# A hybrid decoder block in float32: the first block's first input tile is loaded ahead of the weights, and one retention head moves within block 3

## The chip, the cores and the metric

The kernel runs on one core of a Trainium2 chip. TensorE (PE, with its weight loads PEld), VectorE (DVE), ScalarE (ACT) and GpSimd (POOL) compute, each an instruction stream that is executed in order; SyncE (SP) issues most of the transfers, ScalarE a few, and both streams of transfers are also issued in order. The metric is the device time of one execution in microseconds, as the median of several runs.

## The reference

```python
n = rms_norm(h, attn_norm_w)
proj = einsum('bsd,dc->bsc', n, w_in)
(gq, gk, gv, gg, ga, gb, rq, rk, rv, rg) = split(proj)
o_gdn = gated_deltanet(gq, gk, gv, gg, ga, gb, ...)   # 4 heads, chunked recurrence over the sequence
o_ret = retention(rq, rk, rv, rg)                      # 4 heads, fixed decay per head
h = h + einsum('bsm,md->bsd', concat([o_gdn, o_ret]), w_out)
n2 = rms_norm(h, mlp_norm_w)
h = h + einsum('bsf,fd->bsd', silu(conv(n2 @ w_up)_g) * conv(n2 @ w_up)_u, w_down)
return rms_norm(h, final_norm_w)
```

The sequence has 2048 rows of 1024 columns, heads have 128 columns, the MLP has 2816 hidden columns. Everything is float32.

## The kernel before

**Products.** Each float32 operand is split into a rounded high part (ACT copies it to float32r) and the rest (DVE subtracts), and each product is three TensorE matmuls: high by high, high by low, low by high. `mm3` (lines 113 to 118) records them, as do lines 399 to 401. The output projection and the MLP are done as seven products of half-size blocks (a Winograd form): `product(i)` (line 907) is one of the seven of the output projection, in the order 1, 2, 6, 7, 5, 3, 4.

**Stages.** The sequence is cut into four blocks of 512 rows. For each block the mixers run (projections, gated DeltaNet, retention), then the output projection with its residual and the second norm. After the four blocks follow the MLP's up products and the MLP's down products.

**The order.** The string `ORDER` (lines 41 to 51) lists the items of the four blocks as they are recorded: a digit for the block, then a name. `pro` loads the block's rows and splits them (`pro2` loads the transposed rows `xT` in four tiles `xk` of two k-slices each, line 382, and makes the scaled split tiles `n1`; `pro1` loads the plain rows and takes their squares). `k0`, `v0`, `q0`, `kq` are retention projections, `a`, `f` DeltaNet projections. `r10` to `r13` are four steps of the DeltaNet recurrence of heads 2 and 3 (`gdn_rec`), each a chain that goes TensorE (`ks`), VectorE (line 717), TensorE (`wps`), VectorE (line 727), TensorE (`sps`), VectorE (line 734). `h3` is `ret_head(3)` (transposes `rtr`, products `rkk` and `rr`), `y3` is `ret_out(3)` (the products `ro`, their copy on ACT and the squares). `g0`, `g1` and `G0`, `G1` are `gated(g, hf)` for the first and second half of a block: VectorE multiplies the gate (line 435), TensorE transposes (`mxt`, line 437), ACT copies the result into `co` or `og` (line 440), and for the second half VectorE makes the sums `co[5]`, `co[6]`, `co[7]`, `co[3]` (lines 442 to 445). `W1` is `product(1)`; it reads the first half of the DeltaNet heads, `W2` the first half of the retention heads, `W6` and later ones the sums. A product loads four weight tiles `wv` (five buffers), splits its operand `wu` for two halves m, and records 24 matmuls `wo`.

**What is done with that order.** The items are recorded in this order, each weight load one item ahead (`load_chunk`, called in `hybrid_block`, lines 140 to 150), and a scheduler in the framework then reorders instructions on every engine by its own estimates, within the dependences. So a change of the recorded order can move instructions that it does not name. In the stage between block 3 and the MLP the scheduler lays the MLP's first input splits (`x_...<-xr`, lines 973 and 974, whose loads `xr` SP issues), the remaining output projection and the MLP's first matmuls (`p`) over each other. `unit` (line 72) hands out fixed-size buffers of a pool.

**Weights at the start.** The first item with weights is `0k0`: 264 columns, four loads `wraw` of two k-slices each (line 293), three buffers, split into eight tiles `wc` (lines 295 and 296).

Of the kernel before, what the change touches and what calls it, by code (L numbers as in the profile page):

```python
# [51 lines left out]
P = 128  # L52
S = 2048
D = 1024
# [1 line left out]
TB = 512  # L56
# [15 lines left out]
def unit(pool, tag, shape, dt=F32, **kw):  # L72

    n = int(np.prod(shape[1:]))
    t = pool.tile([P, U1], dt, tag=tag, name=tag, **kw)[:, :n]
    if len(shape) == 3:
        t = t.rearrange("p (a b) -> p a b", a=shape[1])
    elif len(shape) == 4:
        t = t.rearrange("p (a b c) -> p a b c", a=shape[1], b=shape[2])
    return t  # L80


@with_exitstack
def hybrid_block(ctx, tc, x, xT, w_kq, w_v, w_g, w_rk, w_r0, w_r, w_o, w_u, w_d, cols, rows, fnr, masks, rot, out):
    nc = tc.nc
    PE, ACT, DVE, POOL = nc.tensor, nc.scalar, nc.vector, nc.gpsimd

    cp = ctx.enter_context(tc.tile_pool(name="cp", bufs=1))
    drp = ctx.enter_context(tc.tile_pool(name="drp", bufs=2, space=DRAM))


    NCOL = cols.shape[1]
    base = cp.tile([P, U1], F32, name="base")
    colt = base[:, :NCOL]
    nc.scalar.dma_start(colt, cols)
    n1w = colt[:, 0:8]
    n2w = colt[:, 8:16]
    gcw = colt[:, 16:64].rearrange("p (f t) -> p f t", t=4)
    mcw = colt[:, 64:64 + 132].rearrange("p (f t) -> p f t", t=3)
    gv127 = colt[:, 196:200]  # L100
    epsr = colt[:, 200:204]
    gnw = colt[:, 204:205]
    mhalf = base[:, NCOL:NCOL + 16]
    POOL.memset(mhalf, -0.5)
    o = NCOL + 16
    mhalo = base[:, o:o + 4 * NF].rearrange("p (f t) -> p f t", t=2)
    o += 4 * NF
    sfa = base[:, o:o + 2 * (S // P)].rearrange("p (a b) -> p a b", b=2)
    o += 2 * (S // P)

    gamma = [1.0 - 2.0 ** (-5 - h) for h in range(NH)]

    def mm3(ps, pairs, first=True, chk=False):
        n = len(pairs)
        for i, (ah, al, bh, bl) in enumerate(pairs):
            PE.matmul(ps, ah, bh, start=(first and i == 0), stop=False, skip_group_check=chk)  # L116
            PE.matmul(ps, ah, bl, start=False, stop=False, skip_group_check=chk)  # L117
            PE.matmul(ps, al, bh, start=False, stop=(i == n - 1), skip_group_check=chk)  # L118


    n2d = {(b, kk): drp.tile([2, P, TB], F32, name=f"n2d{b}_{kk}", tag=f"n2d{b}_{kk}", bufs=1)
           for b in range(NB) for kk in range(4)}
    hd = [drp.tile([TB, D], F32, name=f"hd{b}", tag=f"hd{b}", bufs=1) for b in range(NB)]
    wud = {}
    marks = {}
    aud = {(q, i): drp.tile([NP, P, TB], F32, name=f"au{q}_{i}", tag=f"au{q}_{i}", bufs=1)
           for q in range(2) for i in range(1, 8)}

    items = mixers(ctx, tc, base, o, marks, drp, mm3, gamma, mhalf, n1w, n2w, gcw, gv127, epsr, gnw, n2d, hd,
                   x, xT, w_kq, w_v, w_g, w_rk, w_r0, w_r, w_o, rows, masks, rot)  # L130
    ups = mlp_up(ctx, tc, marks, drp, mm3, mcw, mhalo, n2d, wud, aud, w_u)
    seq = []
    for name in ORDER.split():
        seq += [(None, None, None)] if name == "U" else items[int(name[0])][name[1:]]
    load_chunk = items["load"]
    order = [i for i, it in enumerate(seq) if it[0] is not None]
    loaded = {}
    nxt = 0
    done = 0
    for i, it in enumerate(seq):  # L140
        while nxt < len(order) and nxt <= done + LA:
            loaded[order[nxt]] = load_chunk(*seq[order[nxt]][:2])
            nxt += 1
        if it[0] is not None:
            it[2](loaded.pop(i))
            done += 1
        elif it[2] is None:
            next(ups)
        else:
            it[2](None)  # L150
    for _ in ups:
        pass
    mlp_down(tc, marks, drp, mm3, sfa, mhalf, hd, aud, w_d, fnr, out)
# [65 lines left out]
def mixers(ctx, tc, base, base_used, marks, drp, mm3, gamma, mhalf, n1w, n2w, gcw, gv127, epsr, gnw, n2d, hd,  # L219
           x, xT, w_kq, w_v, w_g, w_rk, w_r0, w_r, w_o, rows, masks, rot):  # L220
    nc = tc.nc
# [3 lines left out]
    ap_ = ctx.enter_context(tc.tile_pool(name="ap"))  # L225
# [89 lines left out]
    def al(tag, shape, dt=F32):  # L315
        return unit(ap_, tag, shape, dt, **({"bufs": BUFS[tag]} if tag in BUFS else {}))
# [38 lines left out]
    def A_items(b, st):  # L355
# [22 lines left out]
        def pro2(_):  # L378
            st["n1"] = []
            for kk in range(4):  # L380
                xk = unit(ap_, "xk0", [P, 2, TB], bufs=4) if b == 0 else al("xk", [P, 2, TB])
                nc.sync.dma_start(xk.rearrange("p a t -> p (a t)"), xT[b, kk])
                for i in range(2):
                    k = 2 * kk + i
                    n1 = al("n1", [P, 2, TB], F32R)
                    st["n1"].append(n1)
                    ACT.activation(n1[:, 0], xk[:, i], AF.Copy, scale=n1w[:, k:k + 1])  # L387
                    DVE.scalar_tensor_tensor(n1[:, 1], xk[:, i], n1w[:, k:k + 1], n1[:, 0].bitcast(F32),
                                             op0=ALU.mult, op1=ALU.subtract)
# [481 lines left out]
        def gt(g):  # L871
            return [(("g", g), w_g[g], gates(g))]

        items = {"pro": [(None, None, pro2), (None, None, pro1)], "dec": [(None, None, decays)]}
        for h in range(NH):
            items.update({f"d{h}": [(None, None, dmat(h))], f"a{h}": [(("kq", h), w_kq[h], proj_kq(h))],
# [6 lines left out]
        return items  # L883

    wvc = {}

    def W_items(b):
        C = {}
# [68 lines left out]
    sts = [dict() for _ in range(NB)]  # L957
    items = {b: A_items(b, sts[b]) | W_items(b) for b in range(NB)}
    items["load"] = load_chunk
    return items  # L960


# [372 lines left out]
```

## Time and profile before

| what | value |
|---|---|
| median of 3 runs | 2459.84 us (2457.41 to 2461.82) |
| the profiled execution, whole | 2460.31 us |
| its span, first to last instruction | 2458.5 us |
| TensorE's mean granted clock in it | 0.996 |
| VectorE, ScalarE, GpSimd busy | 65%, 41%, 22% |

The profile is of one execution. In its rows "idle before" is the time that an engine stood still ahead of an instruction, with the instruction that released it; PEclk is the share of TensorE's full clock that was granted. Matmuls overlap, so the duration printed for one is longer than the distance between the starts of two.

### The profile page before, as it was taken

The page shows a single profiled execution, that of the slowest core. Times are in us where ns is not written, and L with a number is a line of the kernel's source. Part 1 is how long each engine was busy: PE and PEld are TensorE (multiplying, and loading weights), DVE is VectorE, ACT ScalarE, POOL GpSimd, SP SyncE. Part 2 cuts the span into 40 slices and gives each one's busy share as a digit, 9 for nine tenths or more (in the row PEclk, how much of TensorE's full clock was granted, in tenths as well). Part 3 has the DMA queues.
Part 4 walks back from the last instruction along what each step waited for, and adds up shares of the span by engine and source line. Part 5 has one row for each costly group of instructions (what it writes and reads, how often), then busy time and mean ns, then how long its engine had stood idle before and what let it go on. Part 6 is the DMA issues. An engine that isn't in the chain of part 4 may idle for free.

```text
span 2458.5 us, 35801 instructions
## 1 busy us (share of the span) xinstructions
PE 2397.2 (98%) x12476; PEld 2016.0 (82%) x12476; DVE 1596.7 (65%) x3157; ACT 998.8 (41%) x2152; POOL 532.7 (22%) x877
## 2 busy tenths in 40 slices
PE   8998899999999999998999999999999999999998
PEld 7887788788888878887888888888888888888887
DVE  5855777444754563447888988896556577454674
ACT  6644535344442552336454344442122234332341
POOL 1354245621047105240000000000000002421030
PEclk9999999999999999999999999999999999999999
DMA  8856589674765656654998878877667778775773
GB/s 327 277 187 218 214 310 343 223 247 175 268 228 180 211 186 222 224 184 181 349 365 313 303 290 300 290 280 250 233 239 258 270 259 281 243 224 156 220 242 112
DMA packets 287477, 607.29 MB, mean 247 GB/s; under 512 B 41088, under 2 KB 121152, under 8 KB 287296
## 3 DMA queue, kind: packets, MB, share of 16 engines
q1 hardware_dynamic: 270720, 590.70, 68.7%
q10 hardware_dynamic: 16576, 14.30, 1.9%
q8 instruction: 98, 1.61, 0.3%
q14 instruction: 83, 0.68, 0.1%
HBM read 405.32 MB, written 199.59 MB: 246 GB/s over the span
## 4 chain that ended last, share of the span: by engine, by line
PE 84%; POOL 5%; DMA 4%; DVE 3%; issue 2%; ACT 2%; SPq 0%; ACTq 0%; POOLq 0%; DVEq 0%
PE p L116 11%; PE p L118 11%; PE p L117 11%; PE d L118 6%; PE d L116 6%; PE d L117 6%; PE tok L399 4%; PE tok L401 4%; PE tok L400 4%; PE chm L116 3%; PE chm L117 3%; PE chm L118 3%; POOL pers L639 2%; POOL pers L637 2%; PE wo L116 2%; PE wo L117 2%
## 5 line engine op out<-in xcount | busy, mean ns | idle before, releaser
L117 PE MATMUL p<-x,wu 128*128 128x512 f32 x1176 | 457.7, 389 | 0.0
L116 PE MATMUL p<-x,wu 128*128 128x512 f32 x1176 | 452.7, 389 | 0.0
L118 PE MATMUL p<-x,wu 128*128 128x512 f32 x1176 | 450.0, 389 | 0.0
L399 PE MATMUL tok<-wc,n 128*128 128x512 f32 (+2 forms) x768 | 276.5, 365 | 19.5 <-ACT n L387 9.6
L400 PE MATMUL tok<-wc,n 128*128 128x512 f32 (+2 forms) x768 | 276.6, 361 | 1.1 <-DVE wc L296 1.1
L401 PE MATMUL tok<-wc,n 128*128 128x512 f32 (+2 forms) x768 | 275.1, 361 | 0.0
L116 PEld LDWEIGHTS p<-x,wu 128*128 128x128 f32 x1176 | 220.8, 188 | 46.4 <-DVE uc L1053 0.4
L118 PEld LDWEIGHTS p<-x,wu 128*128 128x128 f32 x1176 | 220.8, 188 | 45.8
L117 PEld LDWEIGHTS p<-x,wu 128*128 128x128 f32 x1176 | 220.8, 188 | 45.8
L1095 DVE SCALAR_TENSOR_TENSOR acc<-uc,base,acc 128x1023 f32<-128x1023 f32 (+1 forms) x176 | 221.0, 1280 | 39.2 <-ACT acc L1092 38.9
L1053 DVE TENSOR_TENSOR uc<-p,uc 128x512 f32<-128x512 f32 x224 | 153.6, 689 | 134.8 <-PE p L118 131.6
L186 POOL TENSOR_TENSOR vt<-vr 128x512 f32<-128x512 f32 x44 | 66.0, 1504 | 633.0 <-DMA vr<-in_w_d 465.8
L399 PEld LDWEIGHTS tok<-wc,n 128*128 128x128 f32 x768 | 146.1, 191 | 41.0 <-ACT n L387 9.6
L117 PE MATMUL d<-v,uu 128*128 128x512 f32 x448 | 174.3, 389 | 0.0
L118 PE MATMUL d<-v,uu 128*128 128x512 f32 x448 | 174.3, 389 | 0.0
L116 PE MATMUL d<-v,uu 128*128 128x512 f32 x448 | 174.3, 389 | 0.0
L400 PEld LDWEIGHTS tok<-wc,n 128*128 128x128 f32 x768 | 146.5, 191 | 20.8 <-DVE wc L296 1.5
L401 PEld LDWEIGHTS tok<-wc,n 128*128 128x128 f32 x768 | 145.3, 191 | 19.8
L116 PE MATMUL chm<-n,wc 128*128 128x512 f32 x384 | 151.7, 395 | 0.0
L118 PE MATMUL chm<-n,wc 128*128 128x512 f32 x384 | 151.2, 394 | 0.0
L117 PE MATMUL chm<-n,wc 128*128 128x512 f32 x384 | 150.8, 393 | 0.0
L1092 ACT ACTIVATE acc<-uc,base 128x1024 f32<-128x1024 f32 x88 | 97.2, 1144 | 86.2 <-DVE uc L1053 45.1
(250 smaller groups left out, 4723.3 us busy)
## 6 DMA issues: line engine op xcount, KB each, us to landing
wu<-wu SPq DMA_DIRECT2D x308, 512.0 KB, 5.9
wc<-wd SPq DMA_DIRECT2D x168, 512.0 KB, 5.2
wv<-wo SPq DMA_DIRECT2D x84, 512.0 KB, 5.2
wd<-wc SPq DMA_DIRECT2D x60, 512.0 KB, 4.8
ur<-au SPq DMA_DIRECT2D x56, 512.0 KB, 5.5
wur<-in_w_u SPq DMA_DIRECT2D x44, 512.0 KB, 6.5
au<-st SPq DMA_DIRECT2D x88, 256.0 KB, 4.7
vr<-in_w_d SPq DMA_DIRECT2D x77, 256.0 KB, 5.0
```

The costliest lines, as they stand in the source:

```text
L116: PE.matmul(ps, ah, bh, start=(first and i == 0), stop=False, skip_group_check=chk)
L117: PE.matmul(ps, ah, bl, start=False, stop=False, skip_group_check=chk)
L118: PE.matmul(ps, al, bh, start=False, stop=(i == n - 1), skip_group_check=chk)
L186: POOL.tensor_tensor(tt[:, j], a, b_, op=ALU.subtract)
L399: PE.matmul(ps, ah, wh, start=(k == 0), stop=False)
L400: PE.matmul(ps, ah, wl, start=False, stop=False)
L401: PE.matmul(ps, al_, wh, start=False, stop=(k == KT - 1))
L637: POOL.tensor_tensor(tm[:, :, :n], Nb[:, j:j + 1, j + 1:].to_broadcast([P, 8, n]), X[:, :, j:j + 1].to_broadcast([P, 8, n]), op=ALU.mult)
L639: POOL.tensor_tensor(X[:, :, j + 1:], X[:, :, j + 1:], tm[:, :, :n], op=ALU.add)
L1053: add = lambda o, ps, a: DVE.tensor_tensor(o, ps, a, op=ALU.add)
L1092: ACT.activation(acc, u, AF.Copy, scale=mcw[:, ci, 2:3])
L1095: DVE.scalar_tensor_tensor(acc[:, t:], u[:, :T2 - t], w, acc[:, t:], op0=ALU.mult, op1=ALU.add)
```

## The change

Two things are changed. A function `load_first` allocates the first of block 0's four `xk` buffers and issues its load; `hybrid_block` calls it ahead of the loop that records the items and loads the weights, and `pro2` takes that tile in place of loading its own. In `ORDER` the items `3h3 3y3` stand between `3r11` and `3r12`, where they stood behind `2N`.

```diff
-         "2W3 3a3 3c3 3kq 3y1 3f3 3e3 3p0 3l0 3r00 3r01 3r02 3r03 3h2 3y2 3b1 3l1 3r10 3r11 3r12 3r13 "
-         "3g0 2W4 3p1 3G0 2N 3h3 3y3 3g1 3G1 3W1 3W2 3W6 3W7 3W5 3W3 3W4 3N")
+         "2W3 3a3 3c3 3kq 3y1 3f3 3e3 3p0 3l0 3r00 3r01 3r02 3r03 3h2 3y2 3b1 3l1 3r10 3r11 3h3 3y3 3r12 "
+         "3r13 3g0 2W4 3p1 3G0 2N 3g1 3G1 3W1 3W2 3W6 3W7 3W5 3W3 3W4 3N")
...
     ups = mlp_up(ctx, tc, marks, drp, mm3, mcw, mhalo, n2d, wud, aud, w_u)
+    items["first"]()
     seq = []
...
             for kk in range(4):
-                xk = unit(ap_, "xk0", [P, 2, TB], bufs=4) if b == 0 else al("xk", [P, 2, TB])
-                nc.sync.dma_start(xk.rearrange("p a t -> p (a t)"), xT[b, kk])
+                if b == 0 and kk == 0:
+                    xk = first[0]
+                else:
+                    xk = unit(ap_, "xk0", [P, 2, TB], bufs=4) if b == 0 else al("xk", [P, 2, TB])
+                    nc.sync.dma_start(xk.rearrange("p a t -> p (a t)"), xT[b, kk])
...
+    first = []
+
+    def load_first():
+        xk = unit(ap_, "xk0", [P, 2, TB], bufs=4)
+        first.append(xk)
+        nc.sync.dma_start(xk.rearrange("p a t -> p (a t)"), xT[0, 0])
...
+    items["first"] = load_first
```

No instruction is added or removed on TensorE, VectorE, GpSimd or SP; ACT gets two more loads of its function table. What the scheduler makes of it differs in two stretches, the first 90 us and the stretch from 1104 us on, and is the same between.

**SP, the first transfers of the program.** `wraw` are the weight loads of `0k0` (`in_w_rk`) and of `0v0` (`in_w_r`), `xk<-in_xT` the four transposed input tiles, `xk<-in_x` the plain rows, `wvr` and `wx` loads for the output projection. Before:

```order
L293 DMA wraw<-in_w_rk 128x528 x2
L382 DMA xk_198<-in_xT 128x1024
L293 DMA wraw<-in_w_rk 128x528
L382 DMA xk_206<-in_xT 128x1024
L382 DMA xk_214<-in_xT 128x1024
L382 DMA xk_222<-in_xT 128x1024
L293 DMA wraw<-in_w_rk 128x528
L360 DMA xk<-in_x 128x1024
L293 DMA wraw<-in_w_r 128x1024
```

Now:

```order
L896 DMA xk_134<-in_xT 128x1024
L294 DMA wraw<-in_w_rk 128x528 x2
L386 DMA xk_206<-in_xT 128x1024
L294 DMA wraw<-in_w_rk 128x528
L386 DMA xk_214<-in_xT 128x1024
L386 DMA xk_222<-in_xT 128x1024
L361 DMA xk<-in_x 128x1024 x2
L179 DMA wvr<-in_w_o 128x512
L294 DMA wraw<-in_w_rk 128x528
L179 DMA wvr<-in_w_o 128x512
L294 DMA wraw<-in_w_r 128x1024
```

The first input tile stands ahead of the first two weight loads, and the fourth weight load of `0k0` stands behind two loads of plain rows and one `wvr`.

**TensorE, the end of block 3's mixers.** `ro` is the last part of `3y3`, `sps` and `ks` are parts of a recurrence step, `nps` is `2N`; `wo` on `wu_11715` and `wu_11737` is `3W1`, on `wu_11765` and `wu_11782` `3W2`, on `wu_11807` and `wu_11824` `3W6`. Before, behind the whole of `3W1` and the last recurrence step:

```order
L846 MATMUL ro<-rv,Ar 128x128
L847 MATMUL ro<-pers_662,ykq 128x128
L437 MATMUL mxt<-base,mix 128x128 x10
L116 MATMUL wo<-wv,wu_11765 128x512
L117 MATMUL wo<-wv,wu_11765 128x512
L116 MATMUL wo<-wv,wu_11782 128x512
```

Now the products of head 3 stand a step earlier, ahead of the last one and of `3W1`:

```order
L963 MATMUL nps<-base,Cw 128x128 x4
L728 MATMUL wps<-kv,AT 128x128 x2
L736 MATMUL sps<-pers_1350,kv 128x128 x2
L736 MATMUL sps<-pers_1350,AT 128x128 x2
L822 MATMUL rr<-rv,rk 128x128 x4
L850 MATMUL ro<-rv,Ar 128x128
L851 MATMUL ro<-pers_125,ykq 128x128
```

and the last eight transposes of the mixers stand between the end of `3W2` and the start of `3W6`:

```order
L118 MATMUL wo<-wv,wu_11765 128x512
L116 MATMUL wo<-wv,wu_11782 128x512
L117 MATMUL wo<-wv,wu_11782 128x512
L118 MATMUL wo<-wv,wu_11782 128x512
L441 MATMUL mxt<-base,mix 128x128 x8
L116 MATMUL wo<-wv,wu_11807 128x512
L117 MATMUL wo<-wv,wu_11807 128x512
L116 MATMUL wo<-wv,wu_11824 128x512
```

So `3W2`, 24 matmuls, was behind the last transposes and is now ahead of them.

**ACT, the copies of those last transposes.** `co` and `og` are the copies of the transposes, `x_2` and `x_3` splits of the MLP's input, `wu_...<-co` the operands of the products. Before:

```order
L440 ACTIVATE og<-mxt,base 128x256
L440 ACTIVATE co<-mxt 128x256
L973 ACTIVATE x_3_12274<-xr 128x512
L440 ACTIVATE co<-mxt 128x256 x2
L917 ACTIVATE wu_11765<-co 128x512
L917 ACTIVATE wu_11782<-co 128x512
L440 ACTIVATE og<-mxt,base 128x256
```

Now:

```order
L444 ACTIVATE co<-mxt 128x256
L444 ACTIVATE og<-mxt,base 128x256
L444 ACTIVATE co<-mxt 128x256
L985 ACTIVATE x_2_12259<-xr 128x512
L985 ACTIVATE x_3_12274<-xr 128x512
L444 ACTIVATE og<-mxt,base 128x256
L928 ACTIVATE wu_11807<-co 128x512
```

The operand splits of `3W2` (`wu_11765`, `wu_11782`) no longer stand among these copies but ahead of them, and the operand of `3W6` follows the last copy directly.

## Prediction

> **What bounds the kernel now.** I read the page first, then TensorE's waits, then the stretches of time in which they lie. The page:
>
> ```profile
> PE 2397.2 (98%) x12476; PEld 2016.0 (82%) x12476; DVE 1596.7 (65%) x3157; ACT 998.8 (41%) x2152; POOL 532.7 (22%) x877
> ```
>
> TensorE is busy for 98%, so only its 61 us of idle time (2458.5 less 2397.2), and time at a reduced clock, can be won by a change that removes no matmul. The waits of TensorE over the whole span (engine and line, what it waited for, us in total, times, longest), its five largest:
>
> ```profile
> PE tok L399 <- ACT n L387: 9.6, 1, 9.6
> PE sps L732 <- DVE pers L727: 6.4, 11, 0.9
> PE mxt L437 <- DVE mix L435: 5.8, 2, 5.0
> PE tok L399 <- ACT mix L412: 5.4, 1, 5.4
> PE wps L724 <- DVE kv L717: 4.8, 8, 1.4
> ```
>
> The first is the start of the program, the third is mostly one wait at the end of block 3, the second and the last are the DeltaNet recurrence. The change reorders just the start and the end of block 3. The stretch at the end of block 3, cut into the recurrence up to its last `ks`, the part up to the last `ro`, and the part up to the first matmul of `3W6` (length, then busy time of PE, PEld, DVE, ACT, POOL, then PEclk, DMA share, GB/s):
>
> ```profile
> 1104.73:1133.74 29.01, 25.20 (x212) 23.26 (x211) 20.07 (x67) 17.01 (x58) 4.04 (x4) 1.00 0.20 73
> 1133.74:1145.14 11.40, 10.95 (x70) 9.59 (x68) 5.75 (x16) 5.12 (x17) 0.50 (x1) 1.00 0.46 147
> 1145.14:1162.92 17.78, 11.64 (x42) 9.44 (x43) 15.61 (x36) 12.90 (x31) 1.51 (x2) 0.71 0.83 313
> ```
>
> Idle there: 3.8, 0.45 and 6.1 us, together 10.4 us. The third part also ran at a mean clock of 0.71. TensorE's rows in it, and two other gaps with the clock around them:
>
> ```profile
> 1150.18 2.37 PE L437 MATMUL mxt<-base,mix 128*128 128x128 f32 x10 [5.05 <-DVE mix L435]
> 1153.64 0.79 PE L116 MATMUL wo<-wv,wu 128*128 128x512 f32 x1 [1.09 <-ACT wu L917]
> 1158.08 0.43 PE L118 MATMUL wo<-wv,wu 128*128 128x512 f32 x1
> 1158.35 0.40 PE L116 MATMUL wo<-wv,wu 128*128 128x512 f32 x1
> 1158.58 0.40 PE L117 MATMUL wo<-wv,wu 128*128 128x512 f32 x1
> ...
> 151.98 1.13 PE L585 MATMUL kk<-ykq 128*128 128x256 f32 x4 [2.35 <-DVE pers L810]
> 218.32 0.80 PE L399 MATMUL tok<-wc,n 128*128 128x512 f32 x1 [5.43 <-ACT mix L412]
> ```
>
> ```profile
> 150.00:155.00 5.00, 3.02 (x13) 2.56 (x14) 4.53 (x9) 4.87 (x17) 2.30 (x3) 1.00 0.82 321
> 215.00:220.00 5.00, 1.68 (x4) 1.39 (x5) 0.00 (x0) 1.57 (x4) 2.46 (x10) 0.61 0.08 26
> 1150.00:1155.00 5.00, 3.72 (x13) 3.16 (x14) 5.00 (x13) 4.90 (x12) 0.00 (x0) 0.50 0.85 329
> ```
>
> A gap of 2.35 us left the clock at 1.00; gaps of 5.43 and 5.05 us halved it. From 1153.64 to 1158.08 ten `wo` took 4.44 us, where the distance at full clock is 0.23 us (1158.35 to 1158.58): 2.1 us lost. The ten transposes before took 2.37 us, about 1.3 us more than at full clock. So the stretch loses 10.4 + 2.1 + 1.3 = 13.8 us in all.
>
> The Trainium skill (TensorE: Matmul & The Clock Gate, "What's actually happening") says that the clock falls to a half after an idle window of about 3.4 us and comes back after as long a busy one. That fits the gaps above; by it a long gap would cost 1.7 us in slow matmuls where I take 2.1.
>
> **The start.** What the first matmul waits for:
>
> ```profile
> 0.74 0.87 SPq L293 DMA_DIRECT2D wraw<-in_w_rk  x2
> 1.65 7.06 DMA xk<-in_xT
> 3.58 0.73 ACT L295 ACTIVATE wc<-wraw 128x264 fp32r<-128x264 f32 x2 [0.16 <-DMA wraw<-in_w_rk]
> 8.80 1.33 ACT L387 ACTIVATE n<-xk,base 128x512 fp32r<-128x512 f32 x2 [3.04 <-DMA xk<-in_xT]
> 9.57 0.59 PE L399 MATMUL tok<-wc,n 128*128 128x264 f32 x1 [9.57 <-ACT n L387]
> ```
>
> Two weight loads are issued ahead of the input tile; the first is on the chip at 3.5 us, the input tile at 8.7, and the first matmul starts 0.77 us after the split of that tile begins. How late the tile will be when it is first in the queue, the trace does not show, so it is bounded. Below: a transfer of this size needs at least its own bytes. What moved by the microsecond (the last column is GB/s, so kB in each us):
>
> ```profile
> 2.00:3.00 1.00, 0.00 (x0) 0.00 (x0) 0.00 (x0) 0.86 (x1) 1.00 (x8) 1.00 0.86 272
> 3.00:4.00 1.00, 0.00 (x0) 0.00 (x0) 0.00 (x0) 0.84 (x3) 0.37 (x1) 1.00 1.02 326
> 4.00:5.00 1.00, 0.00 (x0) 0.00 (x0) 0.78 (x2) 0.39 (x3) 0.00 (x0) 1.00 0.86 297
> 5.00:6.00 1.00, 0.00 (x0) 0.00 (x0) 0.61 (x2) 0.76 (x3) 0.00 (x0) 1.00 1.05 373
> ```
>
> The tile has 524 kB, reached at 3.7 us. Above: this size takes 8.7 us from issue to landing in the busy queue of the first 30 us, so 9.4 and no gain:
>
> ```profile
> xk<-in_xT SPq DMA_DIRECT2D x5, 512.0 KB, 8.7
> ```
>
> I take the row of the first transfer: the first `wraw` (270 kB) was there at 3.5 us, when some 470 kB had moved, 200 kB more than its own. With the norm weights (105 kB, which ACT issues at the same moment and the split needs) and the same 200 kB, the tile lands at 830 kB, about 4.8 us. Then ACT does the two splits (1.33 us) and only now the first `wc`, whose 270 kB land near 6 us; a 0.4 us split gives a first matmul at 6.7 us, 2.9 us earlier.
>
> The Trainium skill (DMA: Bandwidth & Descriptors, "Issuing engines are not separate DMA queues") speaks against more: transfers of ScalarE and SyncE share the same 16 engines and interleave. By it the 262 kB of masks on ScalarE's queue would be mixed in too, and the tile would land near 5.6 us in place of 4.8.
>
> Part of this is given back. The fourth weight load goes behind two row loads and a `wvr`, 1.31 MB; at the rate of the queue that is 3.2 us.
>
> ```profile
> 10.00:20.00 10.00, 10.00 (x67) 10.00 (x67) 8.20 (x15) 9.11 (x19) 0.23 (x1) 1.00 1.03 407
> 15.19 0.72 ACT L295 ACTIVATE wc<-wraw 128x264 fp32r<-128x264 f32 x2
> 20.66 0.28 PE L399 MATMUL tok<-wc,n 128*128 128x264 f32 x1
> ```
>
> ACT split it at 15.19 without a wait, TensorE needed it at 20.66. Now it is ready at 15.2 + 3.2 + 0.4 = 18.8 at the latest, needed at 20.66 - 2.9 = 17.8: a wait of up to 1.0 us, and I take 0.9. Net **2.0 us**, between 0 and 3.5. The weights of `0v0` move back in the queue too, but each of their loads feeds two k-slices or 5.5 us of matmuls (24 of 0.23), and they are hidden. From some 90 us on all engines have the same order as before up to 1104 us, so nothing gives the 2.0 us back: POOL's chains start from what TensorE delivers and move with it.
>
> **The end of block 3.** Before, `3W2` needs head 3's outputs (`ro`, copy, squares, POOL, gate, transposes, copies, split), all of it in one chain with an idle TensorE. Now head 3 comes a step earlier, and `3W2`, 24 matmuls or 5.5 us, can run while the last recurrence step is finished. That covers the 5.05 us wait and the 1.09 us one. Three things are late next.
>
> (a) *The recurrence.* The head's 2.7 us of products move from behind it into it, but its waits are not between matmuls that could be exchanged: a `wps` waits for line 717 and a `sps` for line 727 as before. VectorE now has the four gate products ahead of line 727 once, and once more ahead of line 717:
>
> ```profile
> 1108.56 1.13 DVE L435 SCALAR_TENSOR_TENSOR mix<-o,pers,mix 128x128 f32<-128x128 f32 x4
> ```
>
> Each time about half of the 1.13 us shows (0.6); once `ks` follows `sps` without transposes between them and waits for line 734 (0.6 us, its duration). One of the old waits is filled (0.5). From 4.25 (3.8 + 0.45) to 5.5 us; the bounds are 3.5 (fills three waits) and 7.
>
> (b) *`3W6` behind the last eight transposes.* Its operand needs their copies and sums. Rows of that chain:
>
> ```profile
> 1151.63 0.38 ACT L440 ACTIVATE co<-mxt 128x256 f32<-128x256 f32 x1
> 1151.89 0.63 ACT L973 ACTIVATE x<-xr 128x512 fp32r<-128x512 f32 x1
> 1152.34 0.42 DVE L442 TENSOR_TENSOR co<-og,co 128x256 f32<-128x256 f32 x1
> 1152.94 1.17 ACT L917 ACTIVATE wu<-co 128x512 fp32r<-128x512 f32 x2
> ```
>
> First copy 0.5 us after the first transpose, three copies 1.0, `x_2` and `x_3` 1.05, the last copy 0.35, four sums 1.4, one split 0.6: 4.9 us, less the 0.9 us that the eight transposes take on TensorE, so a wait of **4.0 us**. It is over the 2.35 us that left the clock alone and under the 5.05 that halved it; I take it as halving, 2.1 us more. Bounds: 2.4 us without any slow clock, if the splits of `x_2` and `x_3` overlap the sums, and 6 + 2.1.
>
> (c) *The tiles `wv`.* `3W2`, `3W6` and `3W7` now follow each other more closely, and three of each product's four weight tiles wait for a buffer that the product before frees. From the buffer's release to its next use there are about 5.7 us in `3W2` (15 of `3W1`'s 24 matmuls are over when the first one is free). Landing takes, in the 30 us and the 80 us around:
>
> ```profile
> wv<-wo SPq DMA_DIRECT2D x8, 512.0 KB, 5.3
> DMA to landing us min/median/max: 3.3/6.3/10.4
> ```
>
> At 5.3 us this hides, at 6.3 it costs 0.6; I take 0.3 us, with 0 and 15 as the ends (rival D).
>
> Sum after: 5.5 + 4.0 + 2.1 + 0.3 = 11.9 us against 13.8, a gain of 1.9. Nothing after it is shorter, since the MLP's up products run without gaps. The two table loads on ACT cost 1.28 us each there, off the path: ACT is busy for 41%.
>
> **Forecast.** 2.0 + 1.9 = 3.9 us less. The profiled execution, 2460.31 us with 1.8 us around its span, would be 2456.4; it is 0.5 above the median of 2459.84, so I predict **2455.9 us**. Its own range is 2452 to 2460.
>
> **Rivals.**
> B, *no long gap is left.* (b) stays at 2.4 us, the clock at 1.00, and the full 2.9 us at the start are kept: 13.8 - 5.5 - 2.4 = 5.9, with 2.9 together 8.8, **2451 us**. For it: the scheduler put 24 matmuls where the gap was. Against: my chain is 4 us with instructions in a fixed order.
> C, *the start does not get earlier.* The tile lands in its old 8.7 us because transfers behind it share the engines, or `0k0` waits out what it won: 0 and 1.9, **2458 us**. Against: the first `wraw` landed 2.8 us after its issue.
> D, *the wait moves to `wv`.* If a tile takes 8.7 us, as this size does in the busy queue of the start, `3W2` waits 3.0 us more and `3W6` and `3W7` about as long: 9 us, and with the halved clock twice 2.1: 13.2 less the 3.9 gained, 9.3 us slower, **2469 us**. It decides from a landing time of about 7 us on (three times 1.3 us eat the gain). For it: a DMA share of 0.83 there and a longest landing of 10.4. Against: before, 23 such loads made TensorE wait for 1.1 us in all.
>
> **How the numbers follow.** Forecast 0.46, B 0.28, C 0.12, D 0.14. What a measurement can tell from no change is 0.2%, 4.9 us, so the border is at 2454.9, one us from my forecast. Of the forecast's 0.46 I count 0.20 as faster and 0.26 as the same; B is faster, C the same, D slower: 0.48, 0.38 and 0.14. The range goes from B's lower side, 2449, to where D begins to show, 2463.
>
> **What would show it.** The start: the first `tok` near 6.7 us, and a wait for `wc` or `wraw` of up to 1 us near 18 us. The end of block 3: no wait of `mxt` for `mix` of 5 us, in its place `wo` waiting for `wu` (line 928 now) some 4 us, once, with PEclk under 1.00 after it. Waits of `wo` for `wv` of more than 2 us would mean D; a first `tok` after 9 us C; a `wo` wait under 2.5 us at full clock B. I am wrong as a whole if TensorE's idle time changes by several us between 90 and 1104 us.

## The result, and the profile after

The changed kernel takes 2467.64 us in the median (2463.43 to 2470.61, 19 runs), the kernel before 2460.35 us on the same chips (2457.41 to 2466.01, 19 runs). The ratio is 1.0029 with a 95% interval of 1.0022 to 1.0035: 7.3 us slower by the medians, where 2455.9 us was predicted and 2449 to 2463 was the range. The profiled execution has a span of 2464.7 us, 6.2 more than before.

The page of the changed kernel, busy time by engine:

```profile
PE 2401.4 (97%) x12476; PEld 2017.5 (82%) x12476; DVE 1593.5 (65%) x3157; ACT 999.9 (41%) x2154; POOL 529.9 (21%) x877
```

TensorE is idle for 63.3 us (2464.7 less 2401.4), 2 more than before, and 4.2 us longer busy with the same matmuls; the mean clock was 0.995 where it was 0.996. Its waits (what it waited for, us in total, times, longest):

```profile
PE tok L403 <- ACT wc L296: 7.7, 1, 7.7
PE wo L116 <- ACT wu L928: 7.2, 3, 4.7
...
PE p L116 <- DVE uc L1065: 3.8, 1, 3.8
...
PE p L116 <- ACT wu L985: 1.3, 1, 1.3
...
PE mxt L441 <- DVE mix L439: 0.8, 1, 0.8
```

The first matmul comes at 7.7 instead of 9.6 us. The 5 us wait of `mxt` for `mix` is gone and `wo` waits 4.7 us for `wu` in its place, as the prediction said. New are waits of `p`, a product of the MLP, which before has in no row: 3.8 us for `uc`, a sum on VectorE, and 1.3 us for `wu`.

Both kernels are cut at the same five places in TensorE's order (ahead of matmul 453 of the trace, 6476, 6792, 7051 and 7550, counted from 0). The windows are the start, the stretch in which TensorE's order is the same, the end of block 3, two parts of the stretch where the last output projection and the first MLP products overlap, and the rest; the columns are as in the prediction. Before:

```profile
0.00:91.20 91.20, 81.63 (x453) 72.23 (x453) 59.74 (x161) 57.28 (x124) 14.45 (x39) 1.00 0.86 316
91.20:1105.20 1014.00, 980.72 (x6025) 837.44 (x6024) 571.60 (x1593) 437.09 (x1224) 385.61 (x713) 1.00 0.66 228
1105.20:1163.80 58.60, 48.21 (x319) 42.57 (x318) 41.95 (x118) 35.91 (x107) 6.05 (x6) 0.91 0.45 165
1163.80:1224.00 60.20, 59.09 (x261) 48.52 (x260) 53.69 (x86) 25.56 (x42) 1.32 (x3) 1.00 0.97 370
1224.00:1333.50 109.50, 109.50 (x500) 90.91 (x499) 98.86 (x139) 57.56 (x87) 10.94 (x15) 1.00 0.87 326
1333.50:2458.50 1125.00, 1118.03 (x4928) 924.37 (x4926) 770.87 (x1066) 385.39 (x571) 114.33 (x101) 1.00 0.73 249
```

Changed:

```profile
0.00:88.50 88.50, 80.82 (x452) 71.47 (x453) 58.71 (x160) 58.24 (x125) 15.05 (x39) 1.00 0.85 319
88.50:1103.70 1015.20, 983.02 (x6025) 839.41 (x6023) 569.47 (x1594) 437.38 (x1225) 384.26 (x713) 0.99 0.66 228
1103.70:1160.90 57.20, 47.87 (x320) 41.65 (x318) 40.80 (x116) 32.88 (x101) 6.17 (x6) 0.95 0.49 179
1160.90:1223.10 62.20, 60.48 (x260) 48.53 (x259) 55.50 (x89) 29.12 (x49) 2.14 (x3) 1.00 0.91 345
1223.10:1340.10 117.00, 111.81 (x500) 91.83 (x499) 99.34 (x137) 56.38 (x85) 9.44 (x15) 0.99 0.84 314
1340.10:2464.70 1124.60, 1117.35 (x4928) 924.58 (x4926) 769.68 (x1065) 385.87 (x571) 112.83 (x101) 1.00 0.72 248
```

By stretch the change is -2.7, +1.2, -1.4, +2.0, +7.5 and -0.4 us. The two stretches that the prediction worked out gain 4.1 us; the overlap stretch (fourth and fifth window, 169.7 us before) is 9.5 us longer, and the prediction has no term for it.

The distances between the starts of TensorE's matmuls there account for 9.4 of it: 4.1 us at one wait for `uc`, 1.6 in eight matmuls at half the clock right behind it, 2.0 at three waits from 1190 to 1192 us and 1.7 at one near 1279 us. The wait for `uc`, on TensorE and, ahead of it, on VectorE (start, us, engine, line, operation, count, in brackets the idle time before and its releaser):

```profile
1228.95 0.51 PE L116 MATMUL p<-x,wu 128*128 128x512 f32 x1 [3.85 <-DVE uc L1065]
```

```profile
1216.49 0.69 DVE L1065 TENSOR_TENSOR uc<-p,uc 128x512 f32<-128x512 f32 x1
1218.47 3.80 DVE L1107 SCALAR_TENSOR_TENSOR acc<-uc,base,acc 128x1023 f32<-128x1023 f32 x3 [1.29 <-ACT acc L1104]
1222.19 0.68 DVE L1035 TENSOR_TENSOR st<-wur 128x512 f32<-128x512 f32 x1
1222.79 0.68 DVE L1035 TENSOR_TENSOR st<-wur,st 128x512 f32<-128x512 f32 x1
1223.39 1.28 DVE L1107 SCALAR_TENSOR_TENSOR acc<-uc,base,acc 128x1022 f32<-128x1022 f32 x1
1224.59 1.29 DVE L986 TENSOR_TENSOR wu<-st,wu 128x512 fp32r<-128x512 f32 x2
1226.27 0.69 DVE L901 TENSOR_TENSOR Cw<-Cw,wx 128x512 f32<-128x512 f32 x1 [0.40 <-DMA wx<-in_x]
1226.88 0.68 DVE L986 TENSOR_TENSOR wu<-st,wu 128x512 fp32r<-128x512 f32 x1
1227.48 0.68 DVE L986 TENSOR_TENSOR wu<-wur,wu 128x512 fp32r<-128x512 f32 x1
1228.20 0.69 DVE L1065 TENSOR_TENSOR uc<-p,uc 128x512 f32<-128x512 f32 x1
```

The product that stands still needs a PSUM bank, and the sum at 1228.20 frees it. Eleven other instructions stand ahead of that sum since the sum at 1216.49: the four `acc` of the group before, operand sums and splits `st` and `wu` for a later group, and a residual sum that waits for its load. The sum is that of `p_12538`. The same one before, directly behind the `acc`:

```profile
1217.69 3.67 DVE L1095 SCALAR_TENSOR_TENSOR acc<-uc,base,acc 128x1023 f32<-128x1023 f32 x3 [1.22 <-ACT acc L1092]
1221.28 0.68 DVE L1023 TENSOR_TENSOR st<-wur 128x512 f32<-128x512 f32 x1
1221.88 1.27 DVE L1095 SCALAR_TENSOR_TENSOR acc<-uc,base,acc 128x1022 f32<-128x1022 f32 x1
1223.08 0.68 DVE L1053 TENSOR_TENSOR uc<-p,uc 128x512 f32<-128x512 f32 x1
```

Neither edit names this place: the scheduler laid the stage anew.

### The profile page after: what moved, and what is told of

It is laid out like the page before. It is cut to its first block, busy times and chain, and to the rows that moved or that the text cites. A ratio compares the mean times of both kernels' runs of the same rounds, so it can differ in the third digit from the quotient of the medians.

```text
span 2464.7 us, 35775 instructions
## 1 busy us (share of the span) xinstructions
PE 2401.4 (97%) x12476; PEld 2017.5 (82%) x12476; DVE 1593.5 (65%) x3157; ACT 999.9 (41%) x2154; POOL 529.9 (21%) x877
## 4 chain that ended last, share of the span: by engine, by line
PE 83%; POOL 5%; DMA 4%; DVE 3%; ACT 2%; issue 2%; SPq 0%; ACTq 0%; POOLq 0%; DVEq 0%
PE p L116 11%; PE p L117 11%; PE p L118 10%; PE d L117 6%; PE d L116 6%; PE d L118 6%; PE tok L403 5%; PE tok L405 5%; PE tok L404 5%; PE chm L116 2%; PE chm L117 2%; POOL pers L643 2%; PE chm L118 2%; POOL pers L641 2%; PE wo L116 2%
## 5 line engine op out<-in xcount | busy, mean ns | idle before, releaser
L1107 DVE SCALAR_TENSOR_TENSOR acc<-uc,base,acc 128x1023 f32<-128x1023 f32 (+1 forms) x176 | 221.0, 1279 | 39.2 <-ACT acc L1104 38.9
```

The source lines that it names most:

```text
L1107: DVE.scalar_tensor_tensor(acc[:, t:], u[:, :T2 - t], w, acc[:, t:], op0=ALU.mult, op1=ALU.add)
```

## The experiments

The theory from these profiles: the two edits gain about what was predicted, and the new plan (the order of the instructions on every engine) of the overlap stretch loses more. The rivals: the early tile itself costs (S), or the moved head does (H). All kernels, with the overlap stretch of their profiles (169.7 us before) and the comparison with the kernel before on the same chip:

| run | overlap stretch, us | median, us | before, us | ratio (95%) |
|---|---|---|---|---|
| changed kernel | 179.2 | 2467.64 | 2460.35 | 1.0029 (1.0022 to 1.0035) |
| e4, changed kernel again | 178.6 | 2467.29 | 2459.65 | 1.0028 (1.0016 to 1.0039) |
| e1, early tile alone | 172.0 | 2462.93 | 2459.65 | 1.0017 (1.0008 to 1.0026) |
| e2, moved head alone | 171.6 | 2461.32 | 2459.65 | 1.0004 (0.9995 to 1.0012) |
| e3, change, sum first | 173.2 | 2462.22 | 2459.65 | 1.0006 (0.9997 to 1.0015) |
| e5, e3 and table early | 172.6 | 2461.20 | 2458.51 | 1.0010 (1.0001 to 1.0019) |
| e6, before, sum first | 176.0 | 2465.52 | 2458.51 | 1.0027 (1.0017 to 1.0037) |
| e7, tile on ScalarE's queue | 171.0 | 2464.23 | 2458.51 | 1.0025 (1.0015 to 1.0034) |
| e8, all on ScalarE's queue | 178.1 | 2471.81 | 2458.51 | 1.0047 (1.0034 to 1.0061) |
| e9, early tile, old plan | 170.0 | 2457.75 | 2459.52 | 0.9997 (0.9988 to 1.0006) |
| e16, e9 again | 169.6 | 2458.48 | 2459.93 | 0.9994 (0.9985 to 1.0004) |
| e15, e9 and table early | 170.0 | 2457.57 | 2459.93 | 0.9992 (0.9983 to 1.0001) |
| e10, change, old plan from `3W6` | 179.4 | 2468.35 | 2459.52 | 1.0038 (1.0024 to 1.0051) |
| e11, e10 and table early | 180.6 | 2466.61 | 2459.52 | 1.0028 (1.0017 to 1.0039) |
| e12, old plan from 1166 us | 173.7 | 2462.14 | 2458.95 | 1.0012 (1.0003 to 1.0020) |
| e13, old plan from 1175 us | 175.3 | 2462.37 | 2458.95 | 1.0015 (1.0006 to 1.0024) |
| e14, old plan from 1186 us | 176.6 | 2464.70 | 2458.95 | 1.0029 (1.0020 to 1.0038) |

**e1 and e2, each edit alone.** e1 is the changed kernel with the old `ORDER`, e2 the kernel before with the new one.

> Only the first tile's early load; the order string is the old one (3h3 3y3 behind 2N). Theory T (the loss of the changed kernel comes from VectorE's order in the first groups of the MLP, where p_12538's sum stands behind ten other instructions): here that sum stands behind one of the four acc instructions, so no wait of p for uc over 1 us; the start keeps its 2.6 us by 76 us, and the end of block 3 keeps the 5 us wait of mxt for mix. Median 2456 to 2459. Rival S (the early tile itself costs, through the gap of 3.00 us at kk near 150 us and the halved clock behind it and at 878 us): 2461 to 2465.

> Only the order string is changed (3h3 3y3 between 3r11 and 3r12); the first tile is loaded where it was. Theory T: the sum of p_12538 stands behind four acc and three st instructions but ahead of the wu and Cw instructions, so p waits for uc by 0 to 2 us instead of 3.85; the end of block 3 shows the 4.7 us wait of wo for wu and gains 1 to 2 us by 1164 us. Median 2458 to 2462. Rival H (the moved head itself costs): the loss of the changed kernel is here in full and, without the 2.6 us of the start, more: 2468 to 2472.

Neither alone has the long wait for `uc`, and neither alone loses the 7 us: e2 is within the noise, e1 3.3 us slower. So H falls as the main cause. In e2 the end of block 3 takes 57.2 us against 58.6, the gain of 1.4 us of the changed kernel. e1 misses its range by 4 us and lies in that of S; e9 follows this up. Though no item of block 3 moved in e1, its plan differs from that of the kernel before in about 500 places of TensorE's order behind 1150 us.

**e3, the suspected place.** One order-only edge: the four `acc` of the first MLP group stand behind the sum of `p_12538`.

```diff
-            add(c21, prod(7), c12)
+            st["z", q, g] = add(c21, prod(7), c12)
...
-        fin()
+        if n == 0:
+            late = fin
+        elif n == 1:
+            with tc.issue_after(st["z", 0, 1].ins):
+                late()
+            fin()
+        else:
+            fin()
```

> The changed kernel with one order added: on VectorE the four acc instructions of the first MLP group stand behind the sum that frees p_12538's bank; the orders are the same up to about 1210 us. Theory T: the wait of 3.85 us and the halved clock behind it (1.7 us) go, 2467.6 less 5.5: 2461 to 2463. Rival Q (VectorE is simply short of time there, and another p waits in its place): 2466 to 2469.

The median falls by 5.1 us against e4 on the same chip, where 5.5 was expected. Its waits of `p` for `uc`, and its windows of the overlap stretch:

```profile
PE p L116 <- DVE uc L1065: 1.2, 2, 0.8
```

```profile
1160.80:1223.40 62.60, 60.45 (x260) 48.50 (x259) 54.07 (x90) 27.31 (x48) 2.23 (x3) 1.00 0.92 344
1223.40:1334.00 110.60, 109.82 (x501) 91.00 (x500) 99.62 (x137) 59.22 (x86) 13.25 (x15) 1.00 0.87 328
```

The second window is 6.4 us shorter than in the changed kernel, 1.1 over before's. With the same two edits, what this one edge changes of the plan is worth 5 us of the 7. Another `p` does wait in the place of the old one, but for 0.8 us, so rival Q falls.

**e4, the changed kernel again.** No edit; its profile is read in the section on the hardware.

> The changed kernel once more, for its profile. If the granted clock falls by where a fixed window of 3.4 us happens to lie on the gaps, the waits of 3.00 us (kk near 150 us), 4.75 us (wo) and 3.85 us (p) come again within 0.2 us, but the halved stretches at 151 and 878 us, behind gaps under 3.4 us, need not. If the gaps alone decide, the same five stretches are halved. Median 2466 to 2469.

The waits of 4.75, 3.85 and 3.00 us came again as 4.75, 3.55 and 2.63, the last two outside the 0.2 us expected. The clock was at a half for 17.1 us in this execution, up to the program's last 4 us, and for as long in that of the kernel before; its span is still 5.5 us longer (2464.0 against 2458.5). So a clock that fell by chance is not what makes the changed kernel slower.

**e5, the function table.** A tiny activation ahead of everything:

```diff
+    ACT.activation(sfa[:, 0], mhalf[:, :2], AF.Copy)
```

> The kernel of e3 with one tiny ScalarE activation recorded ahead of everything, so that ScalarE's function table is loaded before the first tile lands; TensorE's and VectorE's orders are those of e3. Theory L (the table load of 1.28 us that stands between the tile's landing at 4.6 us and its split is on the path of the first matmul): first matmul at 6.4 us instead of 7.7, and the lag at 91 us 1.3 us smaller up to the chance of the halved clock at the start; median 2460 to 2462. Rival W (the first matmul waits for its weights anyway, the first wraw landing at 5.4 us): first matmul at 7.2 us or later.

The first matmul comes at 6.67 us where e3 has 7.85, so theory L holds; that it isn't 6.4 is because the split now waits for the norm weights, which land at 4.95 us. The chain of the changed kernel's start (start, us, what) shows the load (line 391, ahead of the split), beside ScalarE's table load in the kernel before:

```profile
0.74 3.87 DMA xk<-in_xT
4.68 1.28 ACT L391
5.98 1.33 ACT n L391 x2
7.31 0.32 ACT wc L296
7.68 1.25 PE tok L403 x4
```

```profile
2.14 1.28 ACT L295 ACT_TABLE_LOAD   x1 [2.14 <-issue]
```

Before, the load of 1.28 us lay under the first weight transfer. Now ScalarE's first operation is the split of the tile, and the load stands between the tile's landing and its split. The Trainium skill (ScalarE: Activation LUTs, "Step-by-step: what each stage is for") says that a table load is placed right before the first activation that needs it; the traces agree, with 1.28 us.

**e6, the same edge on the kernel before.**

> The kernel before with the order of e3 added (the four acc instructions of the first MLP group behind the sum that frees p_12538's bank). If the order is only a repair of the changed kernel's plan: no gain here, since before has no wait of p for uc there; the plan of the stretch from 1210 us on is made anew and costs 0 to 2 us: 2459 to 2462. If it is a gain in itself: 2454 to 2457.

Slower by 7.0 us, far above the 0 to 2 expected: the plan made anew has waits elsewhere, and the second part of the stretch takes 116.2 us. Its row, and the longest wait in it:

```profile
1222.30:1338.50 116.20, 111.59 (x501) 90.52 (x500) 102.47 (x142) 59.58 (x89) 14.82 (x15) 1.00 0.83 314
```

```profile
1233.54 0.50 PE L116 MATMUL p<-x,wu 128*128 128x512 f32 x1 [1.33 <-DVE uc L1053]
```

So the edge is no improvement in itself. It repairs one plan and spoils another. This kernel has neither edit and loses as much as the changed kernel.

**e7 and e8, the tile on ScalarE's queue** (e7 with the old `ORDER`, e8 with the new one and the edge of e3).

```diff
-        nc.sync.dma_start(xk.rearrange("p a t -> p (a t)"), xT[0, 0])
+        nc.scalar.dma_start(xk.rearrange("p a t -> p (a t)"), xT[0, 0])
```

> Only the first tile's early load, with the old order string, issued by ScalarE instead of SyncE, so that no weight load is behind it and the table load stays under the transfers. First matmul near 5.5 us (tile at 4.7, 0.77 us after the start of its split), 4 us earlier than before. The plan from 1150 us on is that of e1 but for a few instructions: if the plan decides, the stretch from 1164 to 1334 us costs some 2 us here as in e1 and the median is 2457 to 2461.

> Both parts of the change, the tile's load issued by ScalarE, and the order of e3. Start 4 us earlier, end of block 3 1.4 us shorter, the stretch from 1164 to 1334 us 2 to 4 us longer than before by a plan of its own: median 2456 to 2460, so at best a little faster than before. If the plan of that stretch is worse than that: 2461 to 2466.

Both miss. ScalarE's rows in e7:

```profile
5.44 0.35 ACTq L95 DMA_DIRECT2D base<-in_cols  x1
...
11.46 1.95 ACT L391 ACTIVATE n<-xk,base 128x512 fp32r<-128x512 f32 x3 [2.37 <-DMA base<-in_cols]
```

The load of the norm weights was put behind ScalarE's splits, which wait for weights, and the split of the tile needs it: first matmul at 12.2 us. e8 also has a new wait of 4.2 us in the overlap stretch (178.1 us).

**e9, e15 and e16, the early tile with the old plan.** The kernel of e1; from 1150 to some 1390 us every engine is held to the order of the kernel before, by order-only edges between neighbours (`PLAN` lists instructions by their place in the recorded order). e15 adds the line of e5.

```diff
+def pin(tc):
...
+    for e, plan in PLAN.items():
+        seq = [kept[e][int(r)] for r in plan.split()]
+        for p, q in zip(seq, seq[1:]):
+            tc.add_manual_dep(q, p.name, mybir.DependencyInfo(mybir.DependencyClass.NoSync, mybir.DependencyReason.DATA), reason="pin")
...
     mlp_down(tc, marks, drp, mm3, sfa, mhalf, hd, aud, w_d, fnr, out)
+    pin(tc)
```

> The early tile with the old order string (the kernel of e1), and from product 6 of block 3 on all engines held to the order that they have in the kernel before, by order-only edges. Theory P (the loss is made by the plan of the stretch where the last output projection and the first MLP products overlap): 1164 to 1334 us takes 169.7 us as before, not e1's 172.0; first matmul at 7.7 us, so 1.8 us earlier; median 2456.5 to 2458.5. Rival S (the early tile moves the times of events so that the old plan no longer fits, or costs elsewhere): 2460 to 2464 as e1.

> The kernel of e9 (early tile, old order string, plan of before held) with e5's tiny ScalarE activation ahead of everything. Theory P with L: first matmul at 6.7 us, 2.9 us ahead of before, nothing given back behind 1104 us: median 2.9 us under before's, so 2455.5 to 2457.5 beside a before of 2459.5, and under e9's by 0 to 1.5 us. If the start's gain is taken back by chance or by a wait in the first 1104 us: 2457.5 to 2460.

> The kernel of e9 once more, beside e15 on the same chip, so that the median of the early tile with the old plan stands on two sets of runs: 2456.5 to 2458.5 by theory P, 1.8 us under before's; 2460 to 2464 by rival S.

e9's windows of the overlap stretch:

```profile
1165.60:1226.00 60.40, 58.97 (x260) 48.49 (x259) 53.46 (x86) 25.30 (x42) 1.33 (x3) 1.00 0.96 361
1226.00:1335.60 109.60, 109.60 (x501) 90.96 (x500) 98.94 (x139) 57.95 (x87) 10.42 (x15) 1.00 0.89 337
```

With the old plan the stretch is as long as before, and the medians are 1.8, 1.5 and 2.4 us under the kernel before, with first matmuls 2.0, 1.9 and 3.1 us earlier. e9 and e16 lie in their range, e15 0.07 us above its own. With the old plan the early tile shows no cost, so S falls. The gain is too small to be shown against the noise; all three intervals hold 1, e15's only just.

**e10 to e14, the whole change with the old plan.** The same edges on the changed kernel, from the first matmul of `3W6` on (e10, and e11 with the table line), or from what it had started by 1166, 1175 and 1186 us.

> The whole change, and from the first matmul of product 6 on all engines held to the order that they have in the kernel before. Theory P: no wait of p for uc near 1229 us, 1164 to 1334 us within 1 us of before's 169.7, the start 1.8 and the end of block 3 1.4 us ahead: median 2455.5 to 2458. Rival S: the waits come back at other instructions, 2461 to 2466. If neither start nor block 3 gained at all: 2459 to 2460.

> The kernel of e10 with the tiny ScalarE activation of e5 ahead of everything, so that the function table is loaded before the first tile lands. First matmul at 6.7 us as in e5, 1.0 us ahead of e10; median 0 to 1.5 us under e10's, 2454.5 to 2457. If the median isn't under e10's by anything, the microsecond is given back before 1104 us.

> As e10, but the seam between the changed kernel's order and that of the kernel before lies later, at what the changed kernel had started by 1166 us, so product 6 is ahead of the first MLP matmuls. Theory P (the plan behind the seam decides, and e10 lost its 8 us at the seam alone): no wait over 2 us behind 1166 us, 1164 to 1334 us between 169 and 172 us, median 2455.5 to 2459. Rival S (the moved head's times don't fit the old plan wherever the seam lies): waits of p for x or wu of together over 4 us behind it, 2461 to 2468.

> As e12 with the seam at 1175 us. Theory P: as e12, 2455.5 to 2459, still without the wait of p for uc near 1229 us. Rival S: 2461 to 2468.

> As e12 with the seam at 1186 us, ahead of the cluster of three waits at 1190 to 1192 us. Theory P: as e12, 2455.5 to 2459. If it is only here that the waits go, the changed plan up to 1186 us is needed; if the stretch is as long as in the changed kernel (178.6), the plan behind 1186 us isn't the cause.

All five miss the range of theory P; e12 and e13 lie in that of rival S. e10's windows, and its wait:

```profile
1161.30:1231.10 69.80, 61.00 (x260) 49.58 (x259) 55.55 (x88) 28.24 (x48) 1.32 (x3) 0.95 0.86 314
1231.10:1340.70 109.60, 109.60 (x501) 90.96 (x500) 99.24 (x140) 58.39 (x87) 10.40 (x15) 1.00 0.88 336
```

```profile
1172.61 0.80 PE L135 MATMUL p<-x,wu 128*128 128x512 f32 x1 [7.87 <-ACT x L1005]
```

The second window is before's 109.5 us again, without a wait, and it is 109.6 in e12, e13 and e14 too: with the old order both edits lose nothing there. But at the seam the loss is in another place: MLP products wait for their input splits `x`, 7.87 us in e10, and at the longest 1.77, 1.43 and 4.10 us in e12, e13 and e14. VectorE may have caught up in these waits, together 2.9 us at the least, so they don't show that the plan alone makes all 7.5 us that the changed kernel loses in this window. What is shown for the two edits together is e5's stretch of 172.6 us: at least 6.6 of the 9.5 us belong to the plan. No seam that was tried fits, so a plan in which the moved head keeps its 1.4 us was not found, and whether there is one stays open.

## Why the prediction was wrong, point by point

**The tile's landing: right.** Forecast 4.8 us (the prediction's own rows put its 830 kB at 4.7), measured 4.61 (0.74 and 3.87). By then 830 kB had moved, as in the sum: 57, 132 and 415 kB in the second to fourth microsecond and 0.61 of 371 in the fifth.

**The first matmul: right in direction, 1.0 us off.** Forecast 6.7, measured 7.68. The step "Then ACT does the two splits (1.33 us)" leaves out the function table's load of 1.28 us, which was hidden before and now stands ahead of them; e5 takes it off the path and has 6.67. The two loads that ScalarE has more lie between 55 and 71 us, not at the end of block 3 where the prediction put them, and no wait comes of them.

**The give-back near 18 us: did not come.** There is no wait of `wc` there. Net of the start: 2.0 forecast; 2.7 at 90 us in one profile of the changed kernel, 1.7 in the other. Rival C falls. From there to 1104 us TensorE is idle for 32.2 us where it was 33.3, so the sign of being wrong as a whole did not come.

**The end of block 3: right, in its size partly by luck.** The wait of `mxt` is gone and `wo` waits for `wu`, 4.75 us for a forecast of 4.0, once, with a clock under 1.00 behind it. Gain 1.9 forecast, 1.4 measured, again 1.4 in e2. Two terms are off against each other. The part up to the wait, with the recurrence:

```profile
1103.70:1151.20 47.50, 42.92 (x308) 37.80 (x305) 31.46 (x97) 27.11 (x90) 6.17 (x6) 1.00 0.39 137
```

Idle there are 4.6 us, where (a) has 5.5. Behind the wait twelve `wo` take 5.29 us (1155.99 to 1161.28) in place of 2.7, so (b) costs 4.75 + 2.6 us instead of 4.0 + 2.1. Rival B falls.

**The step that failed:** "Nothing after it is shorter, since the MLP's up products run without gaps." From this the sum took the overlap stretch as unchanged. The order is changed up to some 1390 us on TensorE, and the prediction followed it only to `3W6`. What the runs showed in its place is a term of +9.5 us (+8.9 in e4): one PSUM bank freed late by VectorE, 3.85 us and a halved clock behind it, worth 5.1 us by e3; the rest in smaller waits, three at 1190 to 1192 us and one of 1.34 us near 1279. e9 shows that the early tile with the old plan has none of this, e6 that another plan can lose nearly as much without either edit. Every kernel tried with both edits still loses at least 2.9 of the 9.5 us there, so whether a plan without that loss exists is not shown.

**Rival D** gave 2469 us and is near the measured time by luck: the waits of `wo` for `wv` that it rests on are 0.6 us in all.

**Still open:** of e1's 3.3 us, its overlap stretch explains 2.3, while its early start should have gained 1.8. Its profile has three halved stretches of the clock ahead of 1104 us that e9's has not; with 11 runs, chance and cause can't be told apart there. Why VectorE's order is so sensitive is argued, not shown: from 1154 to 1184 us it is busy for all 30.00 us before and for 29.73 in the changed kernel, so what is put first there makes something else late.

## What to carry to other kernels

Where a scheduler orders the instructions, an edit's cost isn't only at the edit: compare the new order with the old one on every engine to the end, and price each place where a result that frees a buffer has gone behind other work. Where a stage has two engines near full load, hold the old order there by order-only edges, to see what the edit alone does. And when the first operation of an engine changes, look where its table load goes.

## What the runs showed of the hardware

The clock fell at short gaps, in some executions and not in others. In the changed kernel and in e4, the same program, TensorE has the same gaps near 877 us, 0.79 and 1.55 us with four transposes between them. The wait, and the clock behind it (before the last two columns of the windows), in the one:

```profile
877.32 0.50 PE L116 MATMUL wo<-wv,wu 128*128 128x512 f32 x1 [1.55 <-ACT wu L928]
...
878.17 0.63 PE L117 MATMUL wo<-wv,wu 128*128 128x512 f32 x1
...
881.58 0.40 PE L116 MATMUL wo<-wv,wu 128*128 128x512 f32 x1
```

```profile
878.00:881.00 3.00, 3.00 (x9) 2.37 (x9) 1.81 (x6) 0.07 (x1) 1.01 (x1) 0.53 0.00 0
```

and in the other:

```profile
878.68 0.50 PE L116 MATMUL wo<-wv,wu 128*128 128x512 f32 x1 [1.55 <-ACT wu L928]
```

```profile
879.00:882.00 3.00, 3.00 (x14) 2.35 (x13) 1.88 (x7) 0.44 (x3) 1.01 (x1) 1.00 0.01 5
```

Eight matmuls take 3.41 us (878.17 to 881.58) where they take 1.8 at 0.227 us each: 1.6 us lost. The kernel of e2, which is the same as before up to 1104 us, lost it there too, where the kernel before did not; of all 18 profiles 13 show it.

The prediction's rule that a gap of 2.35 us leaves the clock alone was read from one execution and does not hold in general. The same gap ahead of the same `kk`, in e2 and in e9:

```profile
152.14 2.07 PE L585 MATMUL kk<-ykq 128*128 128x256 f32 x4 [2.38 <-DVE pers L810]
```

```profile
150.79 1.13 PE L609 MATMUL kk<-ykq 128*128 128x256 f32 x4 [3.02 <-DVE pers L834]
```

Behind 2.38 us the clock was 0.50 for 3.4 us (the four `kk` take 2.07 us), behind 3.02 us it stayed at 1.00 (1.13 us). So the length of a gap does not decide it alone. In the clock records of all 18 profiles each halved stretch lasts 3.41, 6.83 or 10.24 us, that is one, two or three times 3.41, but for the one into which the end of each program falls. The Trainium skill (TensorE: Matmul & The Clock Gate, "What's actually happening") says that the window in which activity is counted is 3.4 us long and runs free of the kernel's start; the halved stretches agree, and the two profiles of one program fit it. Single profiles are therefore compared here by stretches, and a difference of one or two such losses between two of them is not read as an effect.
